# The layer norm of a convolution module: PSUM banks, column sums and the steps of its output handed out anew

## The chip, the core and the metric

The kernel runs on one core of a Trainium2 chip. The core has five engines with a queue of instructions each, which work side by side and wait for each other by semaphores: TensorE (PE in the profile; its weight loads are PEld), VectorE (DVE), ScalarE (ACT), GpSimd (POOL) and SyncE (SP), which here issues the DMAs. Matrix products land in PSUM, eight banks of 512 fp32 values per partition; everything else lies in SBUF. The metric is device time in microseconds for one execution, lower is better; a kernel is timed in several runs and the median is taken.

## What is computed

A small two-layer model takes 512 new frames of one stream and 64 next frames of another, 576 columns in all, with 1024 features. Layer 0 mixes by a convolution module, layer 1 by attention; each has a SwiGLU feed-forward part (FFN). Cut to what the change touches:

```python
def layernorm(x, g, b):
    mu = jnp.mean(x, axis=-1, keepdims=True)
    xc = x - mu
    return xc * lax.rsqrt(jnp.mean(xc * xc, axis=-1, keepdims=True) + EPS) * g + b

def conv_module(xn, prefix, w_in, b_in, w_dw, b_dw, ln_g, ln_b, w_out, b_out):
    a, gate = jnp.split(xn @ w_in + b_in, 2, axis=-1)
    u = a * jax.nn.sigmoid(gate)
    y = depthwise_conv(concat([prefix, u]), w_dw) + b_dw      # 31 taps
    y = jax.nn.silu(layernorm(y, ln_g, ln_b))
    return y @ w_out + b_out

h = x + conv_module(rmsnorm(x), ...)
h = h + swiglu(rmsnorm(h), w_gu, w_down)                      # FFN of layer 0
...                                                           # layer 1, final norm
```

The mean and the variance run over the features, so no column of the layer norm can be finished before the convolution of all 1024 features is.

## The kernel before

Features lie on the partitions: eight chunks `c` of 128 features, each 128 x 576. For fp32 accuracy every operand of a matrix product is split into a rounded high part and the rest (`zh`, `zl` for activations, `wh`, `wl` for weights), and a product is three matmuls: high by high, low by high, high by low. A product of one chunk with one 128 x 128 block of weights is done for two halves of 288 columns (`HALVES`), so it is six matmuls (`mm_ops`, L576; the matmul itself is L590).

**The convolution.** Chunks 0, 1, 3 and 6 (`ROWS`) are convolved on DVE, ACT and POOL tap by tap, and lie in time order, 608 columns with the gaps between the streams. Chunks 2, 4, 5 and 7 (`POLY`) are convolved on PE as four phases: column 4n + j lies at place n of phase j, 4 x 152 columns. They come back to a row per feature by a DMA to memory and back (`conv_phases`), with the phases still apart.

**The sums of the layer norm.** For the rows a preliminary mean is taken from chunks 0 and 1 (`less_mean`, tile `pk`) and subtracted everywhere (`kneg`, `knegp`). Then PE sums over features with matrices of ones (`sum_to` for the rows, `sum_of` for the phases) into one tile `cl`: the values (`ys` of the rows, `yes` of the phases, and `ye` of chunk 7, which comes last) and their squares. The rows lie in time order, so phase j of them is read with a step of four elements (`in_phase`, L1030).

**z.** From `cl` follow, on ACT and DVE, minus the mean (`nmp`) and the reciprocal deviation (`rp`); PE spreads both over all partitions in time order (`spread_time`: tiles `nm` and `rt` in PSUM). Then for each chunk (L1216 on): add `nm` to `y`, multiply by `rt`, SiLU with gain and bias (ACT), and split into `zh` (ACT) and `zl` (DVE). The additions of chunks 4 to 7 and one multiplication are on POOL, which cannot read PSUM, so ACT first copies `nm` and `rt` to SBUF (`nms`, `r`).

**The output projection.** Eight output tiles `po`, in the order 0, 4, 1, 5, 2, 6, 3, 7 (`w_out_tile`): each takes all eight chunks of z and two banks of PSUM, in turn the pairs `b4`/`b5`, `b2`/`b3`, `b0`/`b1`. Their weights are loaded and split ahead: two tiles' worth lies ready before z does. After them follows the FFN.

**What sets the order.** A planner (`Plan`) takes every step with a cost written beside it and the tags that it reads and writes, and gives each engine a fixed order. The program is planned in sections: the convolution with its layer norm up to z is one, the projection with the FFN the next, so all of z's instructions stand ahead of the projection's on ACT, DVE and POOL. Each section has its own pool of PSUM tiles; a tile of the second pool lies on the banks that some tile of the first had, by the order in which tags are first used, and waits until that tile's readers are done.

Of the kernel before, what the change touches and what calls it, by code (L numbers as in the profile page):

```python
# [63 lines left out]
Z_DVE = (0, 1, 2, 4, 5, 6, 7)  # L64
# [153 lines left out]
def build(tc, xT, vec, st, stp, bdp, wt, ck, cv, w_in, w_out, gu, down, wk, wv, wq, wo, yT, csp, css, kp, ks, vp, vs):  # L218
# [357 lines left out]
    def mm_ops(dst, tag, wi, xkeys, start=True, stop=True, halves=(0, 1), xdeps=None, order=None, keep=False):  # L576

        n = len(xkeys)
        for q, k in enumerate(order or range(n)):
# [15 lines left out]
            deps = xdeps(xk) if xdeps else [xk + ("h",), xk + ("l",)]  # L595
            if isinstance(tag, tuple):
                out = [tag[hf] for hf in halves]
            else:
                out = [tag] if len(halves) == 2 else [(tag, halves[0])]
            op("PE", 3 * len(halves) * pe(HA), f, reads=wkeys(u) + deps, writes=out, group=None if wi < 2 * NC else (wi, halves))  # L600
# [471 lines left out]
    def add(dst, dk, src, sk):  # L1072

        op("DVE", dve(YW), lambda: nc.vector.tensor_tensor(X[dst], X[dst], X[src], op=ALU.add), reads=[sk], writes=[dk], port=True)
# [9 lines left out]
    def rows_sums(c):  # L1084
# [3 lines left out]
        if c in KN[2:]:  # L1088
            add(("ys",), "ys", ("y", c), ("y", c))
        elif c == KN[1]:  # L1090
            op("DVE", dve(YW), lambda: nc.vector.tensor_tensor(tile(("ys",), "ys", (P, YW)), X[("y", a)], X[("y", c)], op=ALU.add), reads=[("y", a), ("y", c)], writes=["ys"], port=True)
# [20 lines left out]
    def sums_less_mean():  # L1112
# [18 lines left out]
        op("DVE", dve(YW, True), lambda: nc.vector.scalar_tensor_tensor(X[("ys",)], X[("kneg",)], float(n), X[("ys",)], op0=ALU.mult, op1=ALU.add), reads=["kneg"], writes=["ys"], port=True)
# [1305 lines left out]
```

## Time and profile before

| | |
|---|---|
| median of 3 runs | 1252.19 us (1252.18 to 1253.08) |
| the profiled execution | 1253.3 us, of which 1251.6 us from the first to the last instruction |
| mean granted TensorE clock | 0.993 |
| PE busy, whole span | 98% |
| stretch from the last convolution matmul (156.9 us) to the first z of which PE makes steady use (184.5 us) | 27.6 us |

How to read the profile: times count from the first instruction. In a timeline a row is a start, a length, the engine, the line of the kernel, the operation, the tiles written and read (buffer numbers left out), and the number of instructions merged in it; in brackets stand the idle time of the engine just before, and whose result ended it. Back-to-back instructions of one engine overlap a little in such rows, so what one costs in a queue is the distance of starts. An fp32 matmul over plain fp32 data shows as two records.

### The profile page before, as it was taken

What the parts mean: (1) busy time and instruction counts of PE and PEld (TensorE: products, weight loads), DVE (VectorE), ACT (ScalarE), POOL (GpSimd) and SP (SyncE); (2) the same over time, 40 slices, a digit from 0 to 9 for tenths busy, and PEclk for the clock granted to TensorE, in tenths of its full rate; (3) what the DMA queues carried; (4) which work ended last, traced back from release to release, by engine and by line L of the source; (5) the groups of instructions that cost most, each with busy time, mean ns of one, the idle gap of its engine ahead of it and who ended that gap; (6) DMA issues with size and microseconds to landing.
All of it is one profiled execution on the core that took longest, in us unless ns stands there. A gap on an engine that the chain in (4) does not pass through costs nothing.

```text
span 1251.6 us, 24395 instructions
## 1 busy us (share of the span) xinstructions
PE 1221.1 (98%) x9026; PEld 1200.6 (96%) x9026; DVE 984.6 (79%) x1577; ACT 971.8 (78%) x1868; POOL 755.7 (60%) x636
## 2 busy tenths in 40 slices
PE   9999969999999999999999999999999999999996
PEld 8999959999999999999999999998999999999996
DVE  7989964977666659987788999999866666689966
ACT  7986354588878889687758999965988888897873
POOL 2986530469776777775304655455786758777633
PEclk9999989999999999999999999999999999999998
DMA  6333312122323323232463232231323233232222
GB/s 194 111 102 101 98 35 84 58 96 84 120 69 102 101 85 97 75 117 72 131 183 98 48 77 63 52 110 37 100 85 119 69 102 101 86 103 85 100 68 76
DMA packets 46455, 115.61 MB, mean 92 GB/s; under 512 B 8832, under 2 KB 18112, under 8 KB 46336
## 3 DMA queue, kind: packets, MB, share of 16 engines
q1 hardware_dynamic: 46336, 114.05, 29.8%
q8 instruction: 71, 1.16, 0.4%
q14 instruction: 48, 0.39, 0.1%
HBM read 99.04 MB, written 6.34 MB: 84 GB/s over the span
## 4 chain that ended last, share of the span: by engine, by line
PE 85%; DVE 6%; ACT 3%; POOL 3%; DMA 1%; issue 1%; SPq 0%; DVEq 0%; POOLq 0%; ACTq 0%
PE j_A L1398 25%; PE j_B L1398 12%; PE pd L590 7%; PE j_C L1398 6%; PE pg L590 5%; PE po L590 4%; PE pq L590 4%; PE b L2176 4%; PE pa L590 4%; PE py L932 3%; PE pw L590 2%; PE b L2112 2%; PE b L2204 2%; POOL S L438 1%; PE pv L1927 1%
## 5 line engine op out<-in xcount | busy, mean ns | idle before, releaser
L508 ACT ACTIVATE wh<-wr 128x512 fp32r<-128x512 f32 (+1 forms) x303 | 184.5, 613 | 47.2 <-PE po L590 22.8
L518 DVE TENSOR_TENSOR wl<-wr,hp 128x512 fp32r<-128x512 f32 (+1 forms) x241 | 158.8, 663 | 53.6 <-ACT hp L513 53.0
L518 DVE TENSOR_TENSOR wl<-S,hp 128x512 fp32r<-128x512 f32 x226 | 152.7, 681 | 39.6 <-ACT hp L513 37.0
L508 ACT ACTIVATE wh<-S 128x512 fp32r<-128x512 f32 x228 | 141.0, 627 | 31.3 <-PE pd L590 10.5
L513 ACT ACTIVATE hp<-wr 128x512 fp32r<-128x512 f32 (+1 forms) x241 | 138.8, 578 | 22.1 <-DVE wl L518 21.4
L513 ACT ACTIVATE hp<-S 128x512 fp32r<-128x512 f32 x226 | 133.5, 594 | 12.9 <-POOL S L438 7.7
L438 POOL TENSOR_TENSOR S<-wr,wr 128x512 f32<-128x512 f32 x57 | 76.5, 1342 | 91.1 <-ACT wh L508 41.3
L1061 POOL TENSOR_TENSOR pacc<-pacc,pr 128x608 f32<-128x608 f32 x60 | 90.7, 1517 | 22.3 <-ACT pr L1058 16.4
L474 POOL TENSOR_TENSOR S<-wr,S 128x512 f32<-128x512 f32 x57 | 77.5, 1361 | 31.9 <-DVE wl L518 18.2
L438 POOL TENSOR_TENSOR S<-wr 128x512 f32<-128x512 f32 x57 | 78.6, 1381 | 27.9 <-DVE wl L518 10.2
L438 POOL TENSOR_TENSOR S<-S,wr 128x512 f32<-128x512 f32 x57 | 77.7, 1365 | 14.5 <-DVE wl L518 7.1
L1575 POOL TENSOR_TENSOR a<-a,r 128x576 f32<-128x576 f32 x44 | 66.9, 1521 | 15.6 <-DVE a L1552 15.6
L1575 POOL TENSOR_TENSOR t<-t,r 128x576 f32<-128x576 f32 x44 | 66.4, 1510 | 9.8 <-ACT t L1546 9.1
L590 PE MATMUL pd<-ap,wh 128*128 128x288 f32 x384 | 66.0, 294 | 0.0
L518 DVE TENSOR_TENSOR wl<-wr,wh 128x512 fp32r<-128x512 f32 x62 | 49.9, 814 | 11.0 <-ACT wh L508 10.9
L1581 DVE TENSOR_TENSOR a<-a,t 128x576 f32<-128x576 f32 x44 | 53.2, 1209 | 6.5 <-ACT t L1579 5.6
L590 PEld LDWEIGHTS pd<-ap,wh 128*128 128x128 f32 x384 | 56.0, 188 | 0.0
L1058 ACT ACTIVATE pr<-u,vecs 128x608 f32<-128x608 f32 x60 | 47.1, 799 | 8.6 <-POOL pacc L1061 8.2
L1546 ACT ACTIVATE t<-j_A 128x288 f32<-128x288 f32 x84 | 34.0, 406 | 24.6 <-PE j_A L1398 22.1
L1044 DVE SCALAR_TENSOR_TENSOR acc<-u,vecs,acc 128x608 f32<-128x608 f32 x56 | 47.7, 851 | 0.7
L1552 DVE TENSOR_TENSOR t<-j_C,t 128x288 f32<-128x288 f32 x42 | 19.2, 456 | 29.0 <-PE j_C L1398 28.9
L1667 DVE TENSOR_TENSOR h<-j_A,h 128x288 f32<-128x288 f32 x60 | 27.2, 455 | 18.7 <-PE j_A L1398 18.2
(857 smaller groups left out, 4560.1 us busy)
## 6 DMA issues: line engine op xcount, KB each, us to landing
wr<-gu SPq DMA_DIRECT2D x88, 512.0 KB, 3.5
wr<-down SPq DMA_DIRECT2D x32, 512.0 KB, 3.6
wr<-w_in SPq DMA_DIRECT2D x15, 512.0 KB, 3.8
wr<-down SPq DMA_DIRECT2D x16, 384.0 KB, 3.1
qd<-qd SPq DMA_DIRECT2D x21, 256.0 KB, 2.9
wr<-w_out SPq DMA_DIRECT2D x8, 512.0 KB, 3.5
wr<-wq SPq DMA_DIRECT2D x8, 512.0 KB, 3.8
wr<-wo SPq DMA_DIRECT2D x16, 256.0 KB, 2.6
```

The costliest lines, as they stand in the source:

```text
L438: eng(e).tensor_tensor(t[:, :n], x[1](), y[1](), op=ALU.subtract if sub else ALU.add)
L474: eng(e).tensor_tensor(v[:, :n], X[("raw", i0)][:, n : 2 * n], v[:, :n], op=ALU.subtract)
L508: nc.scalar.activation(X[("w", u)][0][:, :n], get(), AF.Copy)
L513: nc.scalar.activation(t[:, :n], get(), AF.Copy)
L518: eng(le).tensor_tensor(b[:, :n], get(), a.bitcast(F32)[:, :n], op=ALU.subtract)
L590: nc.tensor.matmul(o[hf], (hi, hi, lo)[j][:, s], (xh, xl, xh)[j], start=(start and q == 0 and j == 0), stop=(stop and q == n - 1 and j == 2),)
L1044: nc.vector.scalar_tensor_tensor(dst, src, wt_, dst, op0=ALU.mult, op1=ALU.add)
L1061: nc.gpsimd.tensor_tensor(X[("pacc", c)], X[("pacc", c)], X[("pr", c, i)], op=ALU.add)
L1398: nc.tensor.matmul(out, a[:, s], b, start=(start and q == 0 and i == 0), stop=(q == len(ops_) - 1 and i == 2), skip_group_check=True,)
L1575: nc.gpsimd.tensor_tensor(X[k], X[k], r, op=ALU.mult)
L1581: op("DVE", dve(T), lambda: nc.vector.tensor_tensor(X[ku], X[ku], X[kg], op=ALU.mult), reads=by_part(tg), writes=by_part(tu), port=True)
L2176: nc.tensor.matmul(zz()[:, a : a + n], X[("trir",) if same else ("oner",)], X[key][:, x, c : c + n], start=False, stop=(i == len(mms) - 1) ...
```

## The change

Four things are changed, all in the convolution section, and a little in how the first projection tile reads z.

**PSUM.** Three tiles named `at_acc`, `at_p1`, `at_p0` are created ahead of all others, which fixes the banks of those tags. `rt` moves from tag `p1` to the two single banks `mask` and `p4`, and the warming matmuls of that place from `p4` to `p1`.

**Sums.** `ys` and the squares of the rows are laid out phase by phase when they are made (the readers on DVE and ACT now read the rows with a step of four, and PE reads without one). The four phases of `yes` and of the squares of the phases are added to one on POOL, and the two pairs of phases of chunk 7 on DVE, so that PE sums one group where it summed four, or two.

**z.** All additions go to DVE, reading `nm` from PSUM; so do all multiplications, a half at a time from the two banks of `rt`; `zl` of chunks 2, 4 and 6 goes to POOL; the copies `nms` and `r` are gone. Chunk 0 goes through multiplication, SiLU and split in halves, and the first projection tile takes its chunk 0 in halves too. Chunks 5 to 7 use the places `u0` to `u2` for `zf`.

**Order.** `nmp` is read from `cl` after the variance's first step on DVE; steps named `next` (no instruction) tell the planner that the next section reads z.

```diff
-Z_DVE = (0, 1, 2, 4, 5, 6, 7)
-ZF_POOL = (4, 5, 6, 7)
+ZL_POOL = (2, 4, 6)
+Z_AT = ("u0", "u1", "u2")
...
+    for tag in ("acc", "p1", "p0"):
+        pp.tile([P, 1024], F32, name=f"at_{tag}", tag=tag)
...
     def stat_rows(x, dep, i):
-        stat([((lambda j=j: sum_to[:, 96 - 32 * j : 224 - 32 * j]), (lambda j=j: in_phase(x(), j))) for j in range(Q)], [dep], i)
-
-    def stat_phases(x, qs, dep, i):
-        stat([((lambda: sum_of), (lambda q=q: x()[:, q, :])) for q in qs], dep, i)
+        stat([((lambda j=j: sum_to[:, 96 - 32 * j : 224 - 32 * j]), (lambda j=j: x()[:, j, :])) for j in range(Q)], [dep], i)
...
+                def pair(key, b=b):
+                    x = X[(key, c)]
+                    o = tile((key + "2", c, b), f"{key}2{b}", (P, QW))
+                    nc.vector.tensor_tensor(o, x[:, 2 * b, :], x[:, 2 * b + 1, :], op=ALU.add)
...
-            stat_phases(lambda: X[("yes",)], range(Q), ["yes"], 0)
-            stat_phases(lambda: X[("sq", a)], range(Q), ["zq0"], 1)
+            for i, (key, tag) in enumerate(((("yes",), "yes"), (("sq", a), "zq0"))):
+                for n in (2, 1):
+                    def f(key=key, n=n):
+                        x = X[key]
+                        nc.gpsimd.tensor_tensor(x[:, 0:n, :], x[:, 0:n, :], x[:, n : 2 * n, :], op=ALU.add)
+                    op("Pool", pool(n * QW), f, writes=[tag])
+                stat([((lambda: sum_of), (lambda key=key: X[key][:, 0, :]))], [tag], i)
...
-            add(("ys",), "ys", ("y", c), ("y", c))
+            add(("ys",), "ys", ("y", c), ("y", c), True)
...
-                nc.tensor.matmul(X[("pk",)][:, 0:QW], sum_to[:, 96 - 32 * j : 224 - 32 * j], in_phase(X[("ys",)], j), start=(j == 0), stop=False, skip_group_check=True)
+                nc.tensor.matmul(X[("pk",)][:, 0:QW], sum_to[:, 96 - 32 * j : 224 - 32 * j], X[("ys",)][:, j, :], start=(j == 0), stop=False, skip_group_check=True)
...
     table("silu_and_others")
+    RT = ("mask", "p4")
     spread_time(("nm",), "nmp", "p0")
-    warm(N_WARM[1])
-    spread_time(("rt",), "rp", "p1")
-    NT, RT = both("p0"), both("p1")
-    op("ACT", act(T, False), lambda: nc.scalar.activation(r, X[("rt",)][:, O0 : O0 + T], AF.Copy), reads=RT, writes=both("r"))
-    if ZF_POOL:
-        op("ACT", act(T, False), lambda: nc.scalar.activation(tile(("nms",), "kneg", (P, YW))[:, :T], X[("nm",)][:, O0 : O0 + T], AF.Copy), reads=NT, writes=["kneg"])
+    warm(N_WARM[1], "p1")
+    spread_time(("rt",), "rp", RT)
+    NT = both("p0")
...
-                e.tensor_tensor(d, y, m, op=ALU.add)
+                nc.vector.tensor_tensor(d, y, m, op=ALU.add)
...
+        def g(hs, c=c):
+            for hf in hs:
+                z = part(X[("zf", c)], (hf,))
+                nc.vector.tensor_tensor(z, full(X[("rt",)])[hf], z, op=ALU.mult)
...
+            eng("Pool" if c in ZL_POOL else "DVE").tensor_tensor(b, part(X[("zf", c)], hs), a.bitcast(F32), op=ALU.subtract)
...
+    for c in range(NC):
+        op("next", 6 * pe(HA) * 2, None, reads=[("z", c, "h"), ("z", c, "l"), ("z", c, "h", 1), ("z", c, "l", 1)], writes=["next"])
...
-        mm_ops(k, tag, wi, [("z", c) for c in range(NC)], xdeps=...)
+        mm_ops(k, tag, wi, [("z", c) for c in range(NC)], apart=() if i else (0,), xdeps=...)
```

The order of instructions differs in few places; elsewhere it is the same row for row, on DVE in particular up to the last convolution of a row.

The first place is PE's sums into `cl`, right behind the last convolution matmul. Before (`sum_to` are the rows, `sum_of` the phases; `yes` and `sq_2` hold chunks 2, 4 and 5, `ye_7` and `sq_7` are chunk 7):

```order
L988 MATMUL cl_1912<-yes_1787,sum_of_101 128x152 x4
L988 MATMUL cl_1912<-sq_2_1381,sum_of_101 128x152 x4
L988 MATMUL cl_1912<-ys_1154,sum_to_102 128x152 x4
L988 MATMUL cl_1912<-sq_0_1309,sum_to_102 128x152 x4
L988 MATMUL cl_1912<-ye_7_1905,sum_of_101 128x152 x2
L988 MATMUL cl_1912<-sq_7_1908,sum_of_101 128x152 x2
L988 MATMUL cl_1912<-ye_7_1905,sum_of_101 128x152 x2
L988 MATMUL cl_1912<-sq_7_1908,sum_of_101 128x152 x2
```

And on PE in the changed kernel, at the same place:

```order
L994 MATMUL cl_1923<-yes_1789,sum_of_101 128x152
L994 MATMUL cl_1923<-ys_1156,sum_to_102 128x152 x4
L994 MATMUL cl_1923<-sq_0_1312,sum_to_102 128x152 x4
L994 MATMUL cl_1923<-sq_2_1384,sum_of_101 128x152
L994 MATMUL cl_1923<-ye2_7_0_1915,sum_of_101 128x152
L994 MATMUL cl_1923<-sq2_7_0_1921,sum_of_101 128x152
L994 MATMUL cl_1923<-ye2_7_1_1931,sum_of_101 128x152
L994 MATMUL cl_1923<-sq2_7_1_1939,sum_of_101 128x152
```

There were 24 sums and there are 14; the sum of the phases' squares has moved behind those of the rows.

The second place is PE's start on the projection, with the semaphores that each row waits for. Before (`po_0_0` is output tile 0, half 0; `zh0` is chunk 0; a wait for DVE_49 is one for a DVE instruction):

```order
L590 MATMUL po_0_0_2083<-zh0_2011,wh032_1588 128x288 [waits Activation_49]
L590 MATMUL po_0_1_2084<-zh0_2011,wh032_1588 128x288 [waits PE_49]
L590 MATMUL po_0_0_2083<-zl0_2012,wh032_1588 128x288 [waits DVE_49]
L590 MATMUL po_0_1_2084<-zl0_2012,wh032_1588 128x288
L590 MATMUL po_0_0_2083<-zh0_2011,wl032_1589 128x288
L590 MATMUL po_0_1_2084<-zh0_2011,wl032_1589 128x288
L590 MATMUL po_4_0_2085<-zh0_2011,wh234_1737 128x288 [waits DVE_49]
```

PE in the changed kernel, from the same matmul on:

```order
L591 MATMUL po_0_0_2097<-zh0_2010,wh032_1591 128x288 [waits Activation_49]
L591 MATMUL po_0_0_2097<-zl0_2011,wh032_1591 128x288 [waits DVE_49]
L591 MATMUL po_0_0_2097<-zh0_2010,wl032_1592 128x288
L591 MATMUL po_0_1_2098<-zh0_2010,wh032_1591 128x288 [waits Activation_49]
L591 MATMUL po_0_1_2098<-zl0_2011,wh032_1591 128x288 [waits DVE_49]
L591 MATMUL po_0_1_2098<-zh0_2010,wl032_1592 128x288
L591 MATMUL po_4_0_2099<-zh0_2010,wh234_1740 128x288 [waits PE_49]
```

Chunk 0 is taken half by half, and the first matmul of tile 4 waits for PE's own warming matmuls where it waited for DVE.

The third place is DVE's queue from the first multiplication of z on, in the changed kernel (`rt_0`, `rt_1` are the two banks of `rt`; before, three whole multiplications stood here and then `zl0`):

```order
L1266 TENSOR_TENSOR zl0_2011<-zf_0_1990,zh0_2010 128x288
L1252 TENSOR_TENSOR zf_2_2006<-rt_0_1984,zf_2_2006 128x288
L1252 TENSOR_TENSOR zf_2_2006<-rt_1_1985,zf_2_2006 128x288
L1244 TENSOR_TENSOR zf_3_2028<-y_3_1462,nm_1948 128x512
L1244 TENSOR_TENSOR zf_3_2028<-y_3_1462,nm_1948 128x64
L1244 TENSOR_TENSOR zf_4_2032<-y_4_1792,nm_1948 128x512
L1244 TENSOR_TENSOR zf_4_2032<-y_4_1792,nm_1948 128x64
L1252 TENSOR_TENSOR zf_3_2028<-rt_0_1984,zf_3_2028 128x288
L1252 TENSOR_TENSOR zf_3_2028<-rt_1_1985,zf_3_2028 128x288
L1252 TENSOR_TENSOR zf_4_2032<-rt_0_1984,zf_4_2032 128x288
L1252 TENSOR_TENSOR zf_4_2032<-rt_1_1985,zf_4_2032 128x288
L1266 TENSOR_TENSOR zl1_2026<-zf_1_1993,zh1_2025 128x576
```

Between the last half of `zl0` and `zl1` stand the multiplications and additions of three later chunks.

More of the change, by code (lines that the diff above doesn't have):

```diff
@@ L593, in f @@
                         )
[L595 to L600, printed above, removed]
+            for hs in [(hf,) for hf in halves] if k in apart else [halves]:
+                deps = xdeps(xk) if xdeps else [xk + ("h",), xk + ("l",)]
+                deps += [xk + (p, 1) for p in "hl"] if 1 in hs else []
+                if isinstance(tag, tuple):
+                    out = [tag[hf] for hf in hs]
+                else:
+                    out = [tag] if len(hs) == 2 else [(tag, hs[0])]
+                op("PE", 3 * len(hs) * pe(HA), lambda f=f, hs=hs: f(hs), reads=wkeys(u) + deps, writes=out, group=None if wi < 2 * NC else (wi, halves))
         if not keep:
@@ L1238, in hi @@
-        def hi(c=c):
-            a, b = (xpool.tile([P, T], F32R, name=f"z{p}{c}", tag=f"x{p}{c}") for p in "hl")
-            X[("z", c)] = by_half((a, b))
-            X[("zt", c)] = (a, b)
-            nc.scalar.activation(a, X[("zf", c)][:, :T], AF.Copy)
-        def lo(c=c):
-            a, b = X[("zt", c)]
-            nc.vector.tensor_tensor(b, X[("zf", c)][:, :T], a.bitcast(F32), op=ALU.subtract)
-        ys = [("yb", c)] + [("y", c, q) for q in range(Q)] if c in POLY else [("y", c)]
-        if c in ZF_POOL:
-            op("Pool", pool(T) + 0.15, f, reads=["kneg"] + ys, writes=[zt])
-        else:
-            op("DVE", 0.8, f, reads=NT + ys, writes=[zt])
@@ new lines, in part, with s, hi @@
+        def part(t, hs):
+            return t[:, HALVES[hs[0]][0] : sum(HALVES[hs[-1]])]
+        def g(hs, c=c):
+            for hf in hs:
+                z = part(X[("zf", c)], (hf,))
+                nc.vector.tensor_tensor(z, full(X[("rt",)])[hf], z, op=ALU.mult)
+        def s(hs, c=c):
+            z = part(X[("zf", c)], hs)
+            nc.scalar.activation(z, z, AF.Silu, scale=col(V_LNG + c), bias=col(V_LNB + c))
+        def hi(hs, c=c):
+            if not hs[0]:
+                X[("zt", c)] = tuple(xpool.tile([P, T], F32R, name=f"z{p}{c}", tag=f"x{p}{c}") for p in "hl")
+                X[("z", c)] = by_half(X[("zt", c)])
+            nc.scalar.activation(part(X[("zt", c)][0], hs), part(X[("zf", c)], hs), AF.Copy)
@@ new lines, in lo @@
+        def lo(hs, c=c):
+            a, b = (part(t, hs) for t in X[("zt", c)])
+            eng("Pool" if c in ZL_POOL else "DVE").tensor_tensor(b, part(X[("zf", c)], hs), a.bitcast(F32), op=ALU.subtract)
+        ys = [("yb", c)] + [("y", c, q) for q in range(Q)] if c in POLY else [("y", c)]
+        op("DVE", 0.82, f, reads=NT + ys, writes=[zt], urgent=c == 0)
+        for hs in halves:
+            n, k = sum(HALVES[h][1] for h in hs), [("zk", c, hs[0])]
+            zh, zl = (("z", c, q) + hs[:1] * bool(hs[0]) for q in "hl")
+            op("DVE", len(hs) * dve(HA), lambda hs=hs, g=g: g(hs), reads=[zt] + [RT[h] for h in hs], writes=k, urgent=c == 0)
+            op("ACT", act(n) + 0.09, lambda hs=hs, s=s: s(hs), reads=["tbl"], writes=k, urgent=c == 0)
+            first = [zh] if hs[0] else [("x", c, "h"), ("x", c, "l"), zh, zl]
+            op("ACT", act(n, False), lambda hs=hs, hi=hi: hi(hs), reads=k + [("z", 0, "h")] * bool(hs[0]), writes=first, urgent=c == 0)
+            e = "Pool" if c in ZL_POOL else "DVE"
+            op(e, cst(e, n), lambda hs=hs, lo=lo: lo(hs), reads=k + [zh], writes=[zl], urgent=c == 0, port=True)
@@ L1790, in w_out_tile @@
         newps(k, tag)
[L1791 removed]
+        mm_ops(k, tag, wi, [("z", c) for c in range(NC)], apart=() if i else (0,), xdeps=lambda xk: [xk + ("h",), xk + ("l",)] + by_part(f"xh{xk[1]}") + by_part(f"xl{xk[1]}"))
         add_h(m, k, tag, V_BOUT + m)
```

70 lines of the change are left out of this document (29 added, 41 removed).

## The prediction

> **What bounds the kernel now.** The page says first which engine to follow:
>
> ```profile
> span 1251.6 us, 24395 instructions
> PE 1221.1 (98%) x9026; PEld 1200.6 (96%) x9026; DVE 984.6 (79%) x1577; ACT 971.8 (78%) x1868; POOL 755.7 (60%) x636
> ```
>
> PE is busy 98% of the span, so a gain is a stretch where PE idles, runs slowly or does work that it need not do. The list of waits puts the longest one inside this layer norm, on the projection's tile 4. Its stretch by windows (busy time of PE, PEld, DVE, ACT, POOL, then granted clock, DMA share, GB/s):
>
> ```profile
> core 0: us, PE busy (x) PEld busy (x) DVE busy (x) ACT busy (x) POOL busy (x), PEclk, DMA share, GB/s
> 174.00:184.40 10.40, 1.32 (x6) 0.85 (x6) 9.36 (x12) 8.53 (x13) 8.94 (x7) 0.71 0.00 0
> 184.40:188.80 4.40, 4.34 (x19) 4.34 (x20) 3.30 (x6) 2.60 (x4) 0.00 (x0) 0.52 0.02 4
> 188.80:198.30 9.50, 9.50 (x74) 9.50 (x73) 2.83 (x5) 3.16 (x5) 0.00 (x0) 1.00 0.17 55
> 198.30:238.70 40.40, 40.40 (x302) 40.19 (x301) 29.58 (x46) 20.03 (x36) 13.25 (x10) 1.00 0.25 79
> ```
>
> PE works 1.3 of 10.4 us, then 4.4 us at a clock of 0.52, then without a gap until tiles 0 and 4 end at 198.3, and through the other six. PE's timeline:
>
> ```profile
> 129.80 27.05 PE L932 MATMUL py<-vt,wm 128*128 128x152 f32 x204
> 156.69 1.20 PE L988 MATMUL cl<-yes,sum_of 128*128 128x152 f32 x8
> 157.73 1.20 PE L988 MATMUL cl<-sq,sum_of 128*128 128x152 f32 x8
> 158.76 2.32 PE L988 MATMUL cl<-ys,sum_to 128*128 128x152 f32 x8
> 160.90 2.34 PE L988 MATMUL cl<-sq,sum_to 128*128 128x152 f32 x8
> 163.06 0.70 PE L988 MATMUL cl<-ye,sum_of 128*128 128x152 f32 x4
> ...
> 164.63 0.68 PE L988 MATMUL cl<-sq,sum_of 128*128 128x152 f32 x4
> 165.86 2.00 PE L1183 MATMUL nm<-nmp,row_of 128*128 128x72 f32 x16 [0.56 <-ACT nmp L1174]
> ...
> 174.15 0.53 PE L590 MATMUL po<-zh,wh 128*128 128x288 f32 x2 [1.10 <-ACT zh L1242]
> ...
> 184.46 0.85 PE L590 MATMUL po<-zh,wh 128*128 128x288 f32 x2 [8.42 <-DVE zf L1230]
> ...
> 187.51 0.68 PE L590 MATMUL po<-zh,wh 128*128 128x288 f32 x2
> 187.99 0.68 PE L590 MATMUL po<-zl,wh 128*128 128x288 f32 x2
> ...
> 190.64 0.43 PE L590 MATMUL po<-zl,wh 128*128 128x288 f32 x2
> 190.91 0.42 PE L590 MATMUL po<-zh,wl 128*128 128x288 f32 x2
> ```
>
> Three stages limit in turn: PE alone up to 165.3 (convolution, sums); the chain through ACT, DVE and PE that makes z's factors; from there DVE. Tile 4 needs only chunk 0, yet waits 8.42 us for a multiplication `zf` on DVE. It is the last one, of chunk 7: its other operand `rt` lies in the banks that tile 4 takes.
>
> **The sums.** Four sums of phases start 1.04 us apart (156.69 to 157.73), 0.26 each; the four of rows read with a step 2.14 (158.76 to 160.90), 0.535 each. Before: 16 x 0.26 + 8 x 0.535 = 8.4 us; the stretch itself, 156.86 to 165.33, is 8.47. After: 6 x 0.26 + 8 x 0.26 = 3.64. Gain **4.83 us**, if the inputs are there. Chunk 7's last:
>
> ```profile
> 156.89 0.66 DVE L942 SCALAR_TENSOR_TENSOR ye<-py,bdq,knegp 128x152 f32<-128x152 f32 x2 [1.49 <-PE py L932]
> ```
>
> They end at 157.55; a square on ACT (0.46) and a pair of additions of some 0.32 behind it make 158.4, and PE takes that last sum at 156.69 + 13 x 0.26 = 160.1: covered by 1.7. POOL's four added additions (304 and 152 columns; its 608 took 1.5 us, so some 2.8 in all) start when its last one ends at 152.6 and are done by 155.4, 1.3 before PE asks. Without that cover each late microsecond is one of the end.
>
> **Reading with a step.** DVE pays for the new layout earlier:
>
> ```profile
> 82.00:114.50 32.50, 32.50 (x236) 31.66 (x234) 32.21 (x42) 20.34 (x32) 25.11 (x18) 1.00 0.34 100
> 82.71 0.79 DVE L1091 TENSOR_TENSOR ys<-y,y 128x608 f32<-128x608 f32 x1
> 109.34 1.49 DVE L1131 SCALAR_TENSOR_TENSOR ys<-kneg,ys 128x608 f32<-128x608 f32 x1
> 112.97 0.79 DVE L1074 TENSOR_TENSOR ys<-ys,y 128x608 f32<-128x608 f32 x1
> 114.48 0.75 DVE L843 TENSOR_TENSOR sg<-pg,r 128x576 f32<-128x576 f32 x1
> 115.38 0.50 PE L590 MATMUL pg<-xh,wh 128*128 128x288 f32 x2 [0.72 <-DVE sg L843]
> ```
>
> DVE is busy 32.21 of 32.50 us ahead of the `sg` for which PE waits at 115.38, and three additions of that stretch now read a row with a step. The price comes from z: of the next fence's additions, one of a row and one of a polynomial chunk, whose phases it reads with a step, fill 169.85 to 171.73, 1.88 us; one of a row alone 173.72 to 174.45, 0.73. So 1.15 against 0.73, 0.42 more for 576 columns, 0.45 for 608. Three are **+1.35 us** on PE's start there. From below: nothing, if two operands from SBUF hide the step; from above twice as much, 2.7. I take the middle, which an operation of this kind showed. PE's shorter sums into `pk` gain nothing: PE would wait for the same `sg`. The fourth such addition, at 153.3, falls before DVE's idle 1.49 us above.
>
> So ACT, which read `cl` first at 165.35 (the start of the chain, t0), does so at 165.35 - 4.83 + 1.35 = **161.85**.
>
> **z.** The rows of DVE's and POOL's queues, the groups of ACT, POOL and DVE (mean ns), and a half product from PSUM elsewhere (L1667):
>
> ```profile
> 169.85 1.96 DVE L1225 TENSOR_TENSOR zf<-y,nm 128x512 f32<-128x512 f32 x4 [0.78 <-ACT nms L1210]
> 171.73 2.07 DVE L1230 TENSOR_TENSOR zf<-rt,zf 128x576 f32<-128x576 f32 x3
> 173.72 0.81 DVE L1225 TENSOR_TENSOR zf<-y,nm 128x512 f32<-128x512 f32 x2
> 174.45 0.75 DVE L1246 TENSOR_TENSOR zl<-zf,zh 128x576 fp32r<-128x576 f32 x1
> 175.12 0.75 DVE L1230 TENSOR_TENSOR zf<-rt,zf 128x576 f32<-128x576 f32 x1
> 176.22 2.86 DVE L1246 TENSOR_TENSOR zl<-zf,zh 128x576 fp32r<-128x576 f32 x2 [0.35 <-ACT zh L1242]
> 176.44 7.18 POOL L1225 TENSOR_TENSOR zf<-y,nms 128x512 f32<-128x512 f32 x6
> L1236 ACT ACTIVATE zf<-zf,vecs 128x576 f32<-128x576 f32 x8 | 6.7, 860 | 3.4 <-DVE zf L1230 3.4
> L1242 ACT ACTIVATE zh<-zf 128x576 fp32r<-128x576 f32 x8 | 5.2, 676 | 0.1
> L1232 POOL TENSOR_TENSOR zf<-zf,r 128x576 f32<-128x576 f32 x1 | 1.8, 1801 | 2.9 <-DVE zf L1225 2.9
> L1667 DVE TENSOR_TENSOR h<-j_A,h 128x288 f32<-128x288 f32 x60 | 27.2, 455 | 18.7 <-PE j_A L1398 18.2
> ```
>
> In a full queue an operation costs about 0.08 less than its length (0.75 at 174.45, next start 0.67 later). So `zl` 0.67, half a product 0.37, half a `zl` 0.38. `nm` was whole at t0 + 2.5; now `nmp` stands behind a DVE step, so t0 + 3.25 (0.6 and its hand-over). DVE then does, up to `zl1`: rows 0, 1, 3 at 0.73; chunks 2 and 4 at 1.15; ten half products; two halves of `zl0`; `zl1`: 2.19 + 2.3 + 3.7 + 0.76 + 0.67 = 9.62, and some 0.4 of hand-overs: `zl1` at t0 + 13.25. By then PE has done 14 of the 96 matmuls of tiles 0 and 4: the six of chunk 0 for each, and two of `zh1`. A pair starts 0.266 apart at full clock (190.64 to 190.91) and 0.48 apart at 0.52. The 82 left take 82 x 0.133 = 10.9, and 1.85 more if PE starts them cold: 4 us of pairs lost 0.214 each before. I assume it does, since it idles about 3.5 us ahead of them. That makes t0 + 26.0. DVE goes on with chunks 5 to 7: additions 1.15 + 0.73 + 1.15, six half products 2.2, three `zl` 2.0, and 1.8 for ACT's SiLU and `zh` of chunk 7: `zl7` at t0 + 22.3, with 24 matmuls (3.2 us) of chunks 6 and 7 to follow, so not late. `zl2`, 4 and 6 on POOL take at most the 1.8 of its product (L1232) each, and none is asked for sooner than 2 us after its `zh`. The same laying out of rows gives 198.0 for before, where the trace has 198.3; with that 0.3, t0 + 26.3 against t0 + 32.95. Gain **6.65 us**: the wait of tile 4 goes, and late next is `zl1`, so some 3.5 of the 8.42 stays.
>
> The rule that speaks against this: the Trainium skill, TensorE: Matmul & The Clock Gate, What's actually happening, has PE fall to half clock after an idle window of about 3.4 us and return after as long of work. The row of 0.52 for 4 us agrees; by the rule a gap of 3.5 us stands on the edge.
>
> The `zl` that move to POOL meet another rule: the Trainium skill, SBUF — State Buffer, SBUF: two separate sides, gives DVE operations with two SBUF inputs and GpSimd operations one exclusive pair of ports, the second waiting for the whole first. The two `zl` at 176.22 took 1.43 each beside POOL's 7.18 us, against 0.75 alone, which agrees. By the rule `zl3` and `zl7` could lose 0.7 each.
>
> **Behind it.** The other six tiles are the same 302 records on a full PE: 40.4 us. Their splits of weights wait on PE. The FFN's entry is the last place that could give time back:
>
> ```profile
> 240.00:260.00 20.00, 20.00 (x150) 19.79 (x149) 19.27 (x33) 12.62 (x25) 6.90 (x5) 1.00 0.26 79
> ```
>
> DVE is nearly full there, yet its work follows PE's tiles and shifts with them, and it idles 17 of the 50 us before (the two rows up to 238.7). I take nothing, up to 2 us (an estimate: a tenth of this row).
>
> **Sum**: -4.83 + 1.35 - 6.65 = **-10.1 us**. The profiled execution took 1253.3, 1.1 above the median of 1252.19: 1243.2 for such a one, **1242.1** for a median.
>
> **Rivals.** *A larger gain*: PE stays warm over the gap (1.85) and the steps cost nothing (1.35): 13.3 less, 1238.9. For it: the gap is 3.5 us at most and holds two matmuls. Against: the clock was 0.71 on average in the first window, whose gap was longer. 15%.
>
> *A smaller gain*: DVE or PE is slower in z than worked out. If all 82 matmuls run at the slow pitch, 82 x 0.24 = 19.7 in place of 12.75 takes 6.9 back; the steps at twice the price 1.35; the FFN's entry up to 2. One or two such things leave 3 to 8.5 us, 1243.7 to 1249. For it: DVE now carries nearly all of z. 22%.
>
> *The wait merely changes its name*: tile 4 starts early, but what follows it waits for `zl1` until t0 + 19.1, where tile 4 started before (184.46). For it: `zl1` stands behind three later chunks' work. Then z gains under 0.8, and with the steps at twice their price 4.83 - 2.7 = 2.1 is left of the rest: 1250, no change. DVE would have to take 6 us longer for the 9.6 us of work ahead of `zl1`. 4%.
>
> *Slower*: z has one producer now, DVE, and PE's last tiles wait for its last `zl`. All else gains 4.83 - 1.35 = 3.5, so the end is as late as before when tiles 0 and 4 end at t0 + 32.95 + 3.5, which is `zl7` (3.2 before that) at t0 + 33.2: 10.9 later than worked out, and 13.4 for 0.2% slower, some 1255. DVE's work in z is 16.9 us (the two sums above), so each operation would cost 1.8 times its row. With all four whole `zl` at 1.43 (3.0 more) and the four stepped additions at twice theirs (4.6 more) I reach 7.6: still a gain of 3. 4%.
>
> **How the numbers follow.** Forecast 55% (gain 8.5 to 12), larger 15%, smaller 22%, none 4%, slower 4%. The range, 1238.7 to 1246.7, holds the forecast, the larger gain and two thirds of the smaller. A measurement of this kernel can tell about 0.2%, 2.5 us, from no change: faster 92%, the same 4%, slower 4%.
>
> **What would show it.** The sums into `cl` take 3.6 us and their stretch begins 1.35 later than 156.7; the wait for `sg` near 115 grows to 2.1 or more; tile 4's first matmul waits for no multiplication; PE's longest idle time ahead of tiles 0 and 4 is 3 to 4 us and ended by `zl1`; a clock near 0.5 behind it; tiles 0 and 4 end near 188.2. Wrong would be a `zl1` later than t0 + 15, or PE waiting again for chunks 3 to 5, or time given back past 228.

## The result, and the profile after

The changed kernel takes 1241.41 us (median of 5 runs, 1241.29 to 1243.08) against 1252.40 (5 runs, 1252.18 to 1253.98): a ratio of 0.9913, 95% interval 0.9899 to 0.9928. The forecast was 1242.1. The profiled execution took 1241.29 us, its span is 12.0 us shorter.

```profile
span 1239.6 us, 24371 instructions
PE 1215.2 (98%) x9006; PEld 1196.2 (96%) x9006; DVE 987.1 (80%) x1596; ACT 972.2 (78%) x1868; POOL 753.8 (61%) x634
```

PE's busy time fell by 5.9 us; the other 6.1 us of the 12.0 were idle time. PE's timeline after, at the places shown of before:

```profile
116.12 0.50 PE L591 MATMUL pg<-xh,wh 128*128 128x288 f32 x2 [1.58 <-DVE sg L849]
...
157.74 0.53 PE L994 MATMUL cl<-yes,sum_of 128*128 128x152 f32 x2
158.11 1.20 PE L994 MATMUL cl<-ys,sum_to 128*128 128x152 f32 x8
159.14 1.20 PE L994 MATMUL cl<-sq,sum_to 128*128 128x152 f32 x8
...
161.21 0.42 PE L994 MATMUL cl<-sq,sum_of 128*128 128x152 f32 x2
161.47 1.72 PE L777 MATMUL warm<-ones 128*128 128x128 f32 x14
...
171.18 0.53 PE L591 MATMUL po<-zh,wh 128*128 128x288 f32 x2
174.75 0.53 PE L591 MATMUL po<-zl,wh 128*128 128x288 f32 x2 [3.04 <-DVE zl L1266]
...
175.64 0.46 PE L591 MATMUL po<-zl,wh 128*128 128x288 f32 x2
175.91 0.68 PE L591 MATMUL po<-zh,wl 128*128 128x288 f32 x2
176.38 0.68 PE L591 MATMUL po<-zh,wh 128*128 128x288 f32 x2
...
179.26 0.45 PE L591 MATMUL po<-zh,wh 128*128 128x288 f32 x2
```

The sums last 157.74 to 161.47, 3.73 us instead of 8.47. The four sums of rows cost what phases cost (1.03 from start to start, before 2.14). Tile 4 waits for nothing; late next is `zl1`, as the bracket at 174.75 says, and the 8.42 us have become 3.04. Pairs of matmuls start 0.27 apart for the first microsecond behind the gap, then 0.48 apart up to 179.26: the low clock comes late, and costs 7 pairs x 0.21 = 1.5 us.

Three rows date the stage: ACT's first read of `cl` (the t0 of the prediction), and the last addition of a projection tile to `h` on DVE, after and before:

```profile
161.66 0.30 ACT L1207 ACTIVATE vs<-cl 128x152 f32<-128x152 f32 x1 [1.81 <-PE cl L994]
```
```profile
226.73 0.93 DVE L741 SCALAR_TENSOR_TENSOR h<-po,vecs,h 128x288 f32<-128x288 f32 x2
```
```profile
237.94 0.94 DVE L738 SCALAR_TENSOR_TENSOR h<-po,vecs,h 128x288 f32<-128x288 f32 x2
```

t0 is 3.7 us earlier (161.66, before 165.35), and from t0 to the last `h` it is 65.07 us instead of 72.59. From there to the end of the span 1012.9 us are left, before 1013.7: nothing is given back. These stretches are compared below, because single runs of one kernel differ by up to 3 us and the stretches by less.

### The profile page after: what moved, and what is told of

Its sections match the earlier page's. It is cut to its first block, busy times and chain, and to the rows that moved or that the text cites. A ratio compares the mean times of both kernels' runs of the same rounds, so it can differ in the third digit from the quotient of the medians.

```text
span 1239.6 us, 24371 instructions
## 1 busy us (share of the span) xinstructions
PE 1215.2 (98%) x9006; PEld 1196.2 (96%) x9006; DVE 987.1 (80%) x1596; ACT 972.2 (78%) x1868; POOL 753.8 (61%) x634
## 4 chain that ended last, share of the span: by engine, by line
PE 86%; DVE 7%; POOL 3%; ACT 2%; issue 1%; DMA 0%; SPq 0%; DVEq 0%; POOLq 0%; ACTq 0%
PE j_A L1420 28%; PE j_B L1420 14%; PE j_C L1420 7%; PE pd L591 7%; PE po L591 4%; PE pq L591 4%; PE b L2198 4%; PE py L938 3%; POOL pacc L1077 3%; PE pw L591 2%; PE pg L591 2%; PE b L2134 2%; PE b L2226 2%; PE pv L1949 1%; PE pa L591 1%
## 5 line engine op out<-in xcount | busy, mean ns | idle before, releaser
L514 ACT ACTIVATE hp<-wr 128x512 fp32r<-128x512 f32 (+1 forms) x241 | 138.7, 577 | 22.2 <-DVE wl L519 21.7
L475 POOL TENSOR_TENSOR S<-wr,S 128x512 f32<-128x512 f32 x57 | 78.9, 1386 | 32.1 <-DVE wl L519 17.6
L1603 DVE TENSOR_TENSOR a<-a,t 128x576 f32<-128x576 f32 x44 | 50.2, 1142 | 6.0 <-ACT t L1601 5.5
```

Source lines behind the costliest of these rows:

```text
L475: eng(e).tensor_tensor(v[:, :n], X[("raw", i0)][:, n : 2 * n], v[:, :n], op=ALU.subtract)
L514: nc.scalar.activation(t[:, :n], get(), AF.Copy)
L1603: op("DVE", dve(T), lambda: nc.vector.tensor_tensor(X[ku], X[ku], X[kg], op=ALU.mult), reads=by_part(tg), writes=by_part(tu), port=True)
```

## The experiments

Ten runs, in three batches, each beside the kernel before on its chip (medians 1252.62, 1252.82 and 1252.83). All in one table. "wait for `sg`" is PE's wait near 115, and "`sg` to t0" the stretch from the row behind it to t0; "t0 to h" is the stretch above; "half clock" is the time near z for which the records of the granted clock have it at half, idle time of PE included. The stretches and the clock are those of one profiled execution of each kernel.

| run | median us | wait for `sg` | `sg` to t0 | t0 | t0 to h | half clock |
|---|---|---|---|---|---|---|
| before | 1252.40 | 0.72 | 49.97 | 165.35 | 72.59 | 10.24 |
| changed kernel | 1241.41 | 1.58 | 45.54 | 161.66 | 65.07 | 3.41 |
| bank_only | 1244.39 | 0.61 | 49.97 | 165.46 | 64.25 | 3.41 |
| sums_only | 1250.61 | 2.65 | 45.53 | 162.91 | 72.98 | 13.65 |
| bank_sums | 1242.25 | 2.79 | 47.04 | 164.64 | 64.23 | 3.41 |
| no_bank | 1250.53 | 1.68 | 45.53 | 161.53 | 73.32 | 10.24 |
| bank_sums_held | 1240.69 | 1.66 | 45.88 | 162.58 | 64.21 | none |
| rows_time | 1242.93 | 0.69 | 47.54 | 163.23 | 66.02 | 6.83 |
| pe_groups_held | 1244.70 | 1.67 | 46.84 | 163.25 | 66.12 | 6.83 |
| zl1_early | 1240.54 | 1.67 | 45.55 | 162.00 | 64.07 | none |
| after_again | 1241.36 | 1.60 | 45.56 | 162.53 | 65.70 | 6.83 |
| after_fill | 1240.50 | 1.66 | 45.41 | 161.88 | 64.02 | none |

t0 alone scatters: in the changed kernel and after_again, the same program, it lies 0.87 apart, and so do the rows behind the wait for `sg` (116.12 and 116.97). From there to t0 the two agree within 0.02, so what happens between the two places is read from that stretch.

### The banks alone, on the kernel before

```diff
+    for tag in ("acc", "p1", "p0"):
+        pp.tile([P, 1024], F32, name=f"at_{tag}", tag=tag)
...
-    warm(N_WARM[1])
-    spread_time(("rt",), "rp", "p1")
-    NT, RT = both("p0"), both("p1")
+    RT = ["mask", "p4"]
+    warm(N_WARM[1], "p1")
+    spread_time(("rt",), "rp", tuple(RT))
+    NT = both("p0")
...
-                nc.vector.tensor_tensor(z, X[("rt",)][:, O0 : O0 + T], z, op=ALU.mult)
+                for hf in range(2):
+                    zz = z[:, HALVES[hf][0] : sum(HALVES[hf])]
+                    nc.vector.tensor_tensor(zz, full(X[("rt",)])[hf], zz, op=ALU.mult)
```

> The kernel before with the PSUM part alone: rt lies on the two single banks mask and p4 (its readers take it in two halves), the tags acc, p1, p0 have their banks fixed as in the change. Sums and the division of z stay as before. Theory A (the wait of tile 4 is the banks' alone; late next is zl1): sums unchanged (8.47 us, t0 165.35), the 8.42 us wait for zf goes, PE then waits for zl1, which ends about 177.7; 82 matmuls x 0.133 and a cold start of 1.5 to 1.85 behind it make tiles 0 and 4 end near 190.3 in place of 198.3: 8.0 us faster, 1244.3. Rival B (the new division of z is needed for it): PE waits again for zl2 to zl6, whose additions POOL makes, and at least half of the 8 us stays: 1248 or more.

Measured: 1244.39 us, ratio 0.9936 (0.9921 to 0.9950). PE in z:

```profile
174.33 0.53 PE L590 MATMUL po<-zh,wh 128*128 128x288 f32 x2 [2.06 <-ACT zh L1252]
175.57 0.52 PE L590 MATMUL po<-zl,wh 128*128 128x288 f32 x2 [0.71 <-DVE zl L1256]
...
176.46 0.48 PE L590 MATMUL po<-zl,wh 128*128 128x288 f32 x2
176.73 0.68 PE L590 MATMUL po<-zh,wl 128*128 128x288 f32 x2
177.21 0.68 PE L590 MATMUL po<-zh,wh 128*128 128x288 f32 x2
...
180.09 0.44 PE L590 MATMUL po<-zh,wh 128*128 128x288 f32 x2
```

Theory A, on the number. The wait for `zf` is gone with z divided as before, and t0 to h falls by 8.3 us. PE does not wait for `zl1`, as theory A had it; behind these rows it waits for a `zl` once more, for 0.19 us. The low clock sets in here too, behind idle times of only 2.06 and 0.71 us.

### The change without the banks

```diff
-    for tag in ("acc", "p1", "p0"):
-        pp.tile([P, 1024], F32, name=f"at_{tag}", tag=tag)
...
-    RT = ("mask", "p4")
+    RT = both("p1")
...
-    warm(N_WARM[1], "p1")
-    spread_time(("rt",), "rp", RT)
+    warm(N_WARM[1])
+    spread_time(("rt",), "rp", "p1")
```

> The changed kernel with rt back on the tag p1 (one tile, no fixing of banks); sums and z as in the change. Theory A (the banks make the wait): tile 4 waits for the last multiplication of z (near 181.4) for some 9 to 10 us, the clock falls, tiles 0 and 4 end near 195.3 in place of 187.3: 8 us slower than the changed kernel, 1249.4. Rival B (the wait came from POOL's share of z, which is gone): under 2 us slower, 1243.

```profile
181.97 0.85 PE L591 MATMUL po<-zh,wh 128*128 128x288 f32 x2 [11.55 <-DVE zf L1250]
```

Measured: 1250.53, ratio 0.9982 (0.9972 to 0.9991). Theory A: tile 4 waits 11.55 us for the last multiplication, and t0 to h is 73.32, 8.25 more than in the changed kernel. The same 8.3 us appear when the banks are moved alone and when they alone are left out.

### The sums alone, and both together

The edits are the hunks of the change from `stat_rows` to `less_mean`, on the kernel before and on bank_only.

> The kernel before with the sums part alone: rows laid out by phases, groups added ahead. Theory A: the sums take 3.7 us in place of 8.47, the additions that read with a step cost DVE 0.7 to 1.35 ahead of sg, so cl is first read 3.4 to 4.0 us earlier than 165.35; tile 4 still waits about 8.4 us for zf and all behind shifts along: 1248.2 to 1248.8. Rival B: the earlier z meets nothing later and the wait grows by the gain: 1252.

> Both of the above together, z divided between DVE and POOL as before, nmp read ahead of the variance. Theory A (parts add up, the new division of z is worth nothing or less): 8.0 + 3.7 = 11.7 us faster than before, 1240.7, so level with the changed kernel (1241.4) or up to 1 us ahead of it, zl7 at t0 + 21.5 where the changed kernel has t0 + 22.2. Rival B (the division is a gain of its own): 1243 or more, zl1 later than t0 + 13.

Measured: 1250.61 (0.9986, 0.9976 to 0.9995) and 1242.25 (0.9917, 0.9902 to 0.9932), 1.5 to 2.4 us above theory A. The sums are as short as foretold; the loss lies ahead of them. In sums_only, DVE's queue near 110:

```profile
108.91 1.90 DVE L1143 SCALAR_TENSOR_TENSOR ys<-kneg,ys 128x608 f32<-128x608 f32 x1
112.17 0.79 DVE L1078 TENSOR_TENSOR y<-acc,pacc 128x608 f32<-128x608 f32 x1 [1.35 <-POOL pacc L1071]
```

DVE idles 1.35 us for POOL, which neither before nor after has there. The planner makes one plan for the convolution and z together, so without the change's z steps it ordered the convolution anew. PE's wait for `sg` grew to 2.65 us, and in bank_sums to 2.79, after which the clock was low:

```profile
117.60 0.76 PE L590 MATMUL pg<-xh,wh 128*128 128x288 f32 x2 [2.79 <-DVE sg L845]
118.16 0.68 PE L590 MATMUL pg<-xl,wh 128*128 128x288 f32 x2
118.64 0.68 PE L590 MATMUL pg<-xh,wl 128*128 128x288 f32 x2
```

So as wholes these two runs don't price the sums. From `sg` to t0 sums_only takes 45.53 us, as the changed kernel does, where before took 49.97: that stretch is 4.4 us shorter. (bank_sums takes 47.04, with the low clock just shown.) Next, the order was held.

### Banks and sums, the convolution's order held

As bank_sums, but the steps keep the costs of before, and the added additions ride on the steps of the sums instead of being steps of their own:

```diff
-        op("PE", 1.6, f, reads=["ys"], writes=[kt])
+        op("PE", 2.1, f, reads=["ys"], writes=[kt])
...
+                def fold(key=key):
+                    x = X[key]
+                    for n in (2, 1):
+                        nc.gpsimd.tensor_tensor(x[:, 0:n, :], x[:, 0:n, :], x[:, n : 2 * n, :], op=ALU.add)
+                stat([((lambda: sum_of), (lambda key=key: X[key][:, 0, :]))], [tag], i, ahead=fold, n=Q)
```

> The kernel before with banks and sums, z divided as before, and the costs that order the convolution left as they were, so that its steps keep the order of before (in the runs sums_only and bank_sums the convolution was ordered anew and the wait for sg near 115 grew to 2.7 us, where the changed kernel has 1.6). Theory A (the two parts add up; the new division of z is worth nothing): sg wait 1.6 or less, sums 3.7 to 4.2 us, cl first read at 161.7 to 162.2, tiles 0 and 4 end 25.3 us behind it: 1241.0 to 1241.8, level with the changed kernel. Rival B (the division of z carries 1 us or more of the gain): 1242.5 or more, at a cl read as early.

Measured: 1240.69 (1240.52 to 1240.92), ratio 0.9902 (0.9888 to 0.9915). Theory A: with z divided between DVE and POOL as before it is level with the changed kernel. t0 is 0.4 later than expected, most of it because here the squares of the phases come second in PE's queue (`sg` to t0 is 0.34 longer than in the changed kernel):

```profile
158.92 0.53 PE L992 MATMUL cl<-sq,sum_of 128*128 128x152 f32 x2 [0.49 <-POOL sq L1037]
```

t0 to h is 64.21, the third run with the old division at 64.2; the changed kernel has 65.07. The new division of z, with its halves and its order, gains nothing by itself, and loses 0.9. The idle times are those of bank_only (2.06 and 0.70 us), yet the granted clock stays full (the window's columns are those of the prediction's):

```profile
175.00:180.00 5.00, 4.60 (x33) 4.13 (x33) 5.00 (x7) 3.88 (x6) 5.00 (x5) 1.00 0.01 3
```

With this division the clock costs the end nothing: bank_only and bank_sums have it at half for 3.41 us, this run does not, and the three stretches from t0 to h agree within 0.04 us.

### Rows in time order

```diff
-        op("DVE", dve(YW), lambda: nc.vector.tensor_tensor(X[dst], X[dst], in_phases(X[src]) if phases else X[src], op=ALU.add), reads=[sk], writes=[dk], port=True)
+        op("DVE", dve(YW), lambda: nc.vector.tensor_tensor(X[dst], X[dst], X[src], op=ALU.add), reads=[sk], writes=[dk], port=True)
...
-        stat([((lambda j=j: sum_to[:, 96 - 32 * j : 224 - 32 * j]), (lambda j=j: x()[:, j, :])) for j in range(Q)], [dep], i)
+        stat([((lambda j=j: sum_to[:, 96 - 32 * j : 224 - 32 * j]), (lambda j=j: in_phases(x())[:, j, :])) for j in range(Q)], [dep], i)
```

> The changed kernel with the rows left in time order (DVE and ACT read them without a step, PE reads with one). Theory A (PE's step costs 8 x 0.275, DVE's three stepped additions delay sg by 0.75): sums 3.7 + 2.2 = 5.9 us, sg wait back to 0.7 to 0.9, so 1.45 us slower than the changed kernel: 1242.9. Rival B (DVE's steps cost the end nothing): 2.2 us slower, 1243.6.

```profile
115.69 0.51 PE L591 MATMUL pg<-xh,wh 128*128 128x288 f32 x2 [0.69 <-DVE sg L849]
...
157.41 2.32 PE L994 MATMUL cl<-ys,sum_to 128*128 128x152 f32 x8
159.55 2.35 PE L994 MATMUL cl<-sq,sum_to 128*128 128x152 f32 x8
```

Measured: 1242.93, ratio 0.9919 (0.9906 to 0.9933). The wait for `sg` is that of before, the sums of rows start 2.14 apart again, `sg` to t0 is 2.0 longer than in the changed kernel and t0 1.57 later: theory A. The phases are worth some 1.5 us: 2.0 on PE less what DVE pays. The profiled execution, at 1243.74, lost another 0.95 from t0 to h, where its clock was at half for 6.83 us instead of 3.41.

### Groups added by PE

```diff
...
-                    op("Pool", pool(n * QW), f, writes=[tag])
-                stat([((lambda: sum_of), (lambda key=key: X[key][:, 0, :]))], [tag], i)
+                    op("Pool", pool(n * QW), lambda: None, writes=[tag])
+                stat([((lambda: sum_of), (lambda key=key, q=q: X[key][:, q, :])) for q in range(Q)], [tag], i, n=1)
```

> The changed kernel without POOL's four additions of phases: PE sums four groups each of yes and of the squares, as before; all else in the same order. Theory A (the four additions are hidden): 6 x 0.26 = 1.56 us more on PE, DVE's ys and sq at 154 to 157 faster without POOL beside them (1.78 and 1.42 to 1.27 and 0.79) but that ends in idle time: 1.4 to 1.6 us slower, 1242.9. Rival B (POOL's additions end just as PE asks and hold DVE up, so they cost about what they save): 0.7 us slower or less, 1241.4 to 1242.1.

Measured: 1244.70 (1244.41 to 1245.12), ratio 0.9934 (0.9920 to 0.9947): 3.3 slower than the changed kernel, more than either theory. t0 is 1.59 later, but part of that is its scatter: `sg` to t0 is 1.30 longer, where theory A's six sums make 1.56. So POOL's additions are hidden but for some 0.26. In t0 to h 1.05 more is lost with the same idle times as in the changed kernel, to the low clock, which here lasts 6.83 us instead of 3.41. The rest, some 0.7, lies behind the projection, where the twelve traces differ among themselves by up to 1.4; its cause is open. POOL in the changed kernel:

```profile
153.46 1.38 POOL L1041 TENSOR_TENSOR yes<-yes 128x304 f32<-128x304 f32 x1
154.81 1.86 POOL L1041 TENSOR_TENSOR sq<-sq 128x304 f32<-128x304 f32 x1
156.64 1.05 POOL L1041 TENSOR_TENSOR yes<-yes 128x152 f32<-128x152 f32 x1
157.65 0.50 POOL L1041 TENSOR_TENSOR sq<-sq 128x152 f32<-128x152 f32 x1
```

`yes` is ready at 157.69, and PE begins it at 157.74, so PE was waiting: counted from its row for `sg`, its first sum starts 41.62 us later, and 41.48 in pe_groups_held, which needs no addition of POOL's; and the pair of that sum takes 0.37 to the next one, where the others take 0.26.

### zl1 earlier

```diff
-            op("DVE", len(hs) * dve(HA), lambda hs=hs, g=g: g(hs), reads=[zt] + [RT[h] for h in hs], writes=k, urgent=c == 0)
+            op("DVE", len(hs) * dve(HA), lambda hs=hs, g=g: g(hs), reads=[zt] + [RT[h] for h in hs], writes=k, urgent=c <= 1)
```

and likewise on the other four steps of a chunk.

> The changed kernel with chunk 1 of z marked urgent like chunk 0: zl1 stands ahead of the additions and multiplications of chunks 3 and 4. zl1 at t0 + 10.1 in place of 13.0. Theory A (the gap ahead of zl1 makes the clock fall and costs 1.5 us): longest idle time of PE in z under 1.8, granted clock stays at 1.00, tiles 0 and 4 end at t0 + 24.0 to 25.4 in place of 25.7: 0.3 to 1.7 us faster, 1239.7 to 1241.1. Rival B (zl7 sets the end anyway, or the clock falls all the same): 1241.4 to 1242.5.

The list of PE's waits in this stage (us in total, times, longest):

```profile
PE po L591 <- DVE zl L1266: 1.7, 2, 1.1
...
PE po L591 <- POOL zl L1266: 1.1, 2, 0.6
```

Measured: 1240.54, ratio 0.9901 (0.9888 to 0.9915), and t0 to h 64.07, 1.0 less than in the changed kernel. Theory A: no idle time over 1.14, clock 1.00, and PE ends the 96 matmuls of tiles 0 and 4 at t0 + 24.7, in the changed kernel at t0 + 25.8. The addition of tile 4 to `h` comes no earlier (t0 + 26.0 against 25.7), because DVE has four splits of weights ahead of it; from tile 1 on the additions come 1.0 earlier (t0 + 31.0 against 32.1). PE's idle time in z is also 0.8 us shorter than in the changed kernel, so this run does not part the clock from the wait.

### The gap filled, and the changed kernel again

```diff
+                if dst == ("po", 4) and not q:
+                    for _ in range(18):
+                        nc.tensor.matmul(o[0], hi[:, s], X[xk][0][0], start=True, stop=True)
```

> The changed kernel with 18 idle-filling matmuls (2.4 us, into tile 4's banks, overwritten by its first real one) between PE's chunk 0 of tile 0 and of tile 4, so that PE idles under 1 us ahead of zl1. DVE, ACT and POOL keep their queues. Theory A (the low clock behind the gap costs what it shows, 1.5 us): granted clock 1.00 throughout z, the stretch from the first read of cl to the last h 65.07 - 1.2 to 1.5, so 1240.0. Rival B (with a full clock PE only waits for zl3 to zl7 instead): 0.4 us or less, 1241.0 to 1241.6.

> The changed kernel once more, beside after_fill on the same chip. In the runs so far the same idle times of PE in z were followed by a full clock in one (bank_sums_held: 2.06 and 0.70 us) and by a low one in another (bank_only: 2.06 and 0.71 us). Theory A (the fall hangs on where the gap lies in windows that run by themselves, not on the kernel): the stretch from the first read of cl to the last h of the projection differs from the 65.07 us of the first profile by up to 1 us, with the same rows of idle time. Rival B (the kernel's order fixes it): within 0.1 us of 65.07. Either way 1241.4 within 1.

```profile
170.50 2.53 PE L589 MATMUL po<-zh,wh 128*128 128x288 f32 x18
...
174.98 0.53 PE L594 MATMUL po<-zl,wh 128*128 128x288 f32 x2 [0.89 <-DVE zl L1269]
```
```profile
175.00:180.00 5.00, 4.99 (x35) 4.75 (x36) 5.00 (x11) 2.82 (x5) 1.72 (x1) 1.00 0.00 0
```

after_fill: 1240.50 (1240.35 to 1240.54), ratio 0.9901 (0.9886 to 0.9916). With PE kept at work the clock stays full and t0 to h falls by 1.05 us: between the theories, nearer to A. So of the 1.5 us that the low clock shows, some 1.0 reaches the end. All four runs have a mean granted clock of 0.997 or 0.998, the nine of the changed kernel 0.994 to 0.996. The same matmuls in after_again:

```profile
172.01 0.53 PE L591 MATMUL po<-zh,wh 128*128 128x288 f32 x2
175.59 0.85 PE L591 MATMUL po<-zl,wh 128*128 128x288 f32 x2 [3.05 <-DVE zl L1266]
...
180.49 0.42 PE L591 MATMUL po<-zh,wl 128*128 128x288 f32 x2
```

after_again: 1241.36, t0 to h 65.70. It is the same kernel with the same gap, but the clock is low at once and until 180.49, not from 175.91 to 179.26: theory A, 0.6 us apart. rows_time and pe_groups_held, with the same gap and 6.83 us of half clock as here, have 66.02 and 66.12.

The three fastest, after_fill, zl1_early and bank_sums_held, lie 0.7 to 0.9 us below the changed kernel; the intervals overlap, and the stretch of one trace each, with the granted clock, is what tells them apart. Their gains weren't tried together.

## Why the prediction was right

**The sums.** 4.83 us were forecast, 4.74 came (8.47 less 3.73). The cover was mis-sized: POOL's four additions were put at 2.8 us, done at 155.4 and 1.3 before PE asks; they took 1.38 + 1.86 + 1.05 + 0.50 = 4.8 beside DVE's `ys` and `sq`, and PE waited for `yes`. The cover fell short by some 0.26 (pe_groups_held), and by 0.49 in bank_sums_held, where PE asks earlier for the squares.

**Reading with a step.** 0.45 each, 1.35 in all, were forecast. One row of before, and four of after:

```profile
93.77 2.06 DVE L1074 TENSOR_TENSOR y<-y,kneg 128x608 f32<-128x608 f32 x1
```
```profile
82.55 1.29 DVE L1107 TENSOR_TENSOR ys<-y,y 128x608 f32<-128x608 f32 x1
...
94.07 1.53 DVE L1090 TENSOR_TENSOR y<-y,kneg 128x608 f32<-128x608 f32 x1
...
109.11 1.88 DVE L1149 SCALAR_TENSOR_TENSOR ys<-kneg,ys 128x608 f32<-128x608 f32 x1
...
113.12 1.27 DVE L1090 TENSOR_TENSOR ys<-ys,y 128x608 f32<-128x608 f32 x1
```

They are longer by 0.50, 0.39 and 0.48 (before 0.79, 1.49 and 0.79), 1.37 in sum. But PE started only 0.74 later, and its wait for `sg`, forecast at 2.1 or more, came to 1.58: the addition at 94.07, which reads nothing with a step, takes 0.53 less than before. Probably it falls otherwise beside POOL's additions; in rows_time, without the stepped addition ahead of it, it takes 2.03 again. Another 0.3 us were lost between there and the sums, of which the wait for `yes` is a part. So t0 came to 161.66, forecast 161.85. That it came so near is luck in part: a saving of 0.5 that was not counted, and a t0 that scatters by more than that (162.53 in after_again).

**z.** `zl1` ended at t0 + 13.0 (forecast 13.25) and `zl7` at t0 + 22.2 (22.3); the gap is 3.04 us (3 to 4), ended by `zl1`; the low clock cost 1.5 (1.85). So PE ended tiles 0 and 4 at t0 + 25.8 (26.3), and the forecast gain of 6.65 is 7.5 by t0 to h. The 0.7 us that `zl3` and `zl7` could have lost beside POOL did not come (0.75 and 0.76 long); the two rows that the prediction read as 1.43 each were 0.87 and 2.07. What the prediction didn't separate is what earns it: the banks alone take 8.3, and the new division of z, whose queue it laid out operation by operation, takes back 0.9, about what after_fill shows the clock behind its gap to cost (1.05). The prediction's mechanism, that the wait of tile 4 goes and `zl1` is late next, is right. What it did not see is that the low clock behind the gap costs the end something only with the new division.

**Behind it.** Nothing was given back, as forecast.

**The sum.** -10.1 was forecast from a profiled execution that lay 1.1 above its median; the medians differ by 11.0. The two profiled executions differ by 12.0: 3.7 up to t0, 7.5 from there to the last `h`, and 0.8 behind it, which is within what that last stretch differs from trace to trace. Of the rivals, the larger gain (a clock that stays full, 1.85) had its mechanism right and its size too large: 1.05. The rule of the Trainium skill, TensorE: Matmul & The Clock Gate, What's actually happening, which puts the fall behind an idle window of about 3.4 us, is too mild here: 2.06 and 0.71 us with matmuls between them sufficed in bank_only. Its other statement, that the window runs freely and the point of the change therefore varies from run to run, is what after and after_again show.

## What to carry to other kernels

Where PE waits for an operation that produces nothing it reads, look at which PSUM banks its output takes and who read them last: moving one tile to other banks was worth 8.3 of the 11 us, the shorter sums 3 to 4, and the new division of z less than nothing. When one part of a change is run alone under a planner, compare the order of everything else first, since the rest may have been planned anew. Ask of a gap on PE not only how long it is but what the clock does behind it: filling it with idle matmuls recovered 1.05 us here. Before two kernels are compared by a time mark, see how far that mark moves between two runs of one kernel.

## What the hardware showed beyond that

A gap of 2 to 3 us in PE's work may or may not bring the low clock. With 2.06 and 0.71 us it fell in bank_only, with 2.05 and 0.70 in bank_sums, and with 2.06 and 0.70 it did not in bank_sums_held; with 2.79 it fell in bank_sums, with 2.65 in sums_only it did not; with 3.04 it fell in all four traces with that gap, for 3.41 us in one and for 6.83 in three.

The records of the granted clock say more. In each of the twelve traces every stretch at full or at half clock, between the first and the last of the execution, is a whole number of steps of 3.41 us (1 to 4 at half, 16 to 360 at full), and where the steps lie differs from run to run. So one and the same gap is cut by the steps in different ways. Steps in bank_only, then in bank_sums_held:

```profile
173.27:176.68 3.41, 1.64 (x10) 1.41 (x11) 3.25 (x9) 3.38 (x6) 1.70 (x1) 1.00 0.02 5
176.68:180.09 3.41, 3.41 (x16) 3.41 (x15) 3.41 (x4) 2.93 (x5) 3.41 (x4) 0.50 0.00 0
```
```profile
167.57:170.99 3.42, 1.82 (x16) 1.62 (x15) 3.42 (x10) 1.56 (x3) 1.42 (x2) 1.00 0.44 153
170.99:174.40 3.41, 2.25 (x14) 1.92 (x14) 3.25 (x7) 3.41 (x6) 2.30 (x2) 1.00 0.00 0
174.40:177.81 3.41, 3.19 (x22) 2.82 (x22) 3.41 (x5) 2.81 (x5) 3.41 (x3) 1.00 0.02 5
```

In bank_only PE is busy for 1.64 us of one step, and the next runs at half; in bank_sums_held the same idle time is split over two steps with 1.82 and 2.25. The twelve traces have some 4200 steps at full clock, without the first and last 15 us. The nine in which PE is busy for less than 0.49 of the step are all followed by one at half clock (1.64 of 3.41, the step of bank_only, is 0.48); of all others one is, at 0.57 in after_again. So here it was the busy share of a step that counted, and not the length of a gap; why the step of 0.57 stands out is open. This comparison was made after the runs, and no run moved a gap against the steps on purpose.

The two profiled executions of the changed kernel, 1241.29 and 1242.16, differ by 0.87 up to t0, by 0.63 from t0 to h, which is the clock's, and by 0.6 the other way behind it. What makes the first and the last, and the wider scatter of single runs, wasn't traced.
